# Gate and up of two SwiGLU stages as seven block products in place of eight, with feed-forward groups of six tiles

## The chip, the core and the metric

The kernel runs on one core of a Trainium2 chip. The metric is the device time of one execution in microseconds (us). The core has five engines that run side by side: TensorE (PE, matrix products; its weight loads are listed apart as PEld), VectorE (DVE, elementwise), ScalarE (ACT, activation functions and copies), GpSimd (POOL) and SyncE (SP, which here issues the loads from HBM). SBUF is the working memory, PSUM (eight banks of 128 x 512 f32) takes the matrix products.

## What is computed

A decoder trunk of two layers on 512 tokens with 1024 channels: a convolution module, attention into 256 memory tokens and a SwiGLU stage in layer 0; differential attention, memory attention and a SwiGLU stage in layer 1; a final RMSNorm. The part that the change is about is the SwiGLU stage, which both layers have:

```python
def swiglu(h, w_gate, w_up, w_down):
    return (jax.nn.silu(h @ w_gate) * (h @ w_up)) @ w_down

# in each layer i, with norm_ffn a gain per channel:
x = x + swiglu(rms_norm(x, norm_ffn[i]), ffn_w_gate[i], ffn_w_up[i], ffn_w_down[i])
```

Here h is 512 x 1024, w_gate and w_up are 1024 x 2816 and w_down is 2816 x 1024. The hidden width 2816 makes 22 tiles of 128. RMS normalisation multiplies each token by a factor r that depends on the token alone, and each channel by its gain.

## The kernel before

The residual stream lies transposed in SBUF as eight tiles `xT[t]`, 128 channels x 512 tokens. A matrix product of f32 values is made from three products of rounded values: `split` (lines 219 to 223) and `weights` (lines 208 to 217) divide a tile into a high part, cast by ACT, and a low part, the difference, made by DVE or (with `lo=G`) by POOL. `mm3` (lines 231 to 234) then multiplies high by high, high by low and low by high into the same PSUM bank. So a product of a 128 x 128 weight tile with a 128 x 512 activation tile is three matmuls, each with a weight load of its own.

The stages follow each other as `conformer` (phases c, c2), `memory_attention(0)` (m0), `ffn0` (f0), `diff_attention` (d), `memory_attention(1)` (m1) and `ffn1` (f1), lines 1041 to 1052. Each phase has its own plan of SBUF slots and PSUM banks (lines 69 to 96): a name in `SLOTS` or `BIG` owns a ring of buffers, and a buffer is used again when its last reader is done. The order of the instructions on each engine is made when the program is built, by a planner that simulates the program's time line (line 1092); `tc.issue_after` and `tc.keep_in_program_order` bind it. Each engine then works through its own list in order: an instruction that waits holds up all that stand behind it on that engine.

A SwiGLU stage before the change: `residual_out` (lines 340 to 347) ends the memory attention. For each of its eight output tiles it adds to `xT[m]`, squares for the norm and splits gain times `xT[m]` into `xg`; `norm.finish()` sums the squares over channels on PE, takes the root (small DVE operations, `rsqrt_sums`), and spreads the factor over the partitions on PE (`R`). `gate_up` (lines 622 to 634) takes `xg` without the token factor and multiplies by `R` afterwards: for each hidden tile t, 24 matmuls of 512 columns for gate and 24 for up, with a load of 512 KB each, then on DVE gate times R, up times R, their product with Silu, and a split into `a`. The 22 tiles go in groups of 8, 8 and 6 (`FFN_GROUPS`, line 37). After each group `ffn0` multiplies its part of w_down and adds to `xT`; `ffn1` does the same with tokens on the partitions (`xo`, transposed once after the first group), and ends with the final norm and the stores. In f0 the first group is followed in program order by `rotary_tables`, `minus_lambda` and `half_masks` (lines 639 to 642), which `diff_attention` needs later.

Of the kernel before, what the change touches and what calls it, by code (L numbers as in the profile page):

```python
# [17 lines left out]
AF = mybir.ActivationFunctionType  # L18
# [4 lines left out]
P = 128  # L23
# [13 lines left out]
FFN_GROUPS = [list(range(0, 8)), list(range(8, 16)), list(range(16, 22))]  # L37
# [10 lines left out]
def _pieces(value, bits, count):  # L48
# [23 lines left out]
MEMB = {"e": 4, "sq": 1, "mo": 16}  # L72
FFN0B = {"tg": 3, "sg": 3, "tu": 4, "ta": 4, "sq": 2, "ctab": 2, "stab": "ctab", "lq": 2, "lpr": "lq", **TABLES}
FFNB = {"tg": 3, "sg": 3, "tu": 4, "ta": 4, "sq": 2, "gf": 2, "xo": 8}
# [3 lines left out]
    "c": CONV, "c2": CONV, "m0": {"mkf": 8, **MEMB}, "m1": {"fetch": 4, **MEMB}, "f0": FFN0B, "f1": FFNB,  # L78
# [3 lines left out]
FFNG = {"st": 4, "wh": 3, "wl": 3, "a": 11}  # L82
# [7 lines left out]
FFNP = {"": "01234567"}  # L90
# [9 lines left out]
def trunk(ctx, tc, xt, memt, rows, taps, pos, norm_final, conv_w_pw1, conv_w_pw2, w_k_shared, w_v_shared,  # L100
# [99 lines left out]
    def pc(name, i=0):  # L200
        c = COL[name] + i
        return prm[:, c:c + 1]
# [16 lines left out]
    def split(src, name, shape=(P, 512), lo=None):  # L219
        h, l = pair(name, shape)  # L220
        A.copy(h, src)  # L221
        (lo or V).tensor_tensor(l, src, f(h), op=ALU.subtract)  # L222
        return h, l
# [17 lines left out]
    def at(pair, *idx):  # L241
        return pair[0][idx], pair[1][idx]
# [51 lines left out]
    def broadcast_rows(r, ps):  # L294

        for i in range(NB):
            ins = T.transpose(ps[:, i * P:(i + 1) * P], r[:, i:i + 1].to_broadcast([P, P]), ident)
        return ins.ins
# [41 lines left out]
    def residual_out(W, ins, norm, bias=None, cols=1, lo=None):  # L340
# [6 lines left out]
        norm.finish()  # L347
# [218 lines left out]
    def memory_attention(L, n, nxt):  # L566
        sc = small("sc", [P, NB])
        V.tensor_scalar(sc, n.r, 1.0 / 16.0, None, op0=ALU.mult)
        o, mv = [], []

# [48 lines left out]
        residual_out(mem_w_o[L], o, nxt)  # L619


    def gate_up(L, n, fts):
        a = []
        for t in fts:
            pg, pu = bank("gu"), bank("gu")
            linear(ffn_w_gate[L], t, n.xs, pg, lo=G)
            linear(ffn_w_up[L], t, n.xs, pu)
            tg, sg, tu, ta = tl("tg"), tl("sg"), tl("tu"), tl("ta")
            V.tensor_tensor(tg, pg, n.R, op=ALU.mult)  # L629
            A.activation(sg, tg, AF.Silu)  # L630
            V.tensor_tensor(tu, pu, n.R, op=ALU.mult)  # L631
            V.tensor_tensor(ta, tu, sg, op=ALU.mult)
            a.append(split(ta, "a"))
        return a

    def ffn0(n, nxt):
        for fts in FFN_GROUPS:
            a = gate_up(0, n, fts)
            if fts is FFN_GROUPS[0]:
                cur["tables"] = rotary_tables()  # L640
                cur["nlam"] = minus_lambda()
                cur["halves"] = half_masks()
            for m in range(KT):
                ps = bank("down")
                linear(ffn_w_down[0][fts[0] * P:(fts[-1] + 1) * P, :], m, a, ps)
                V.tensor_tensor(xT[m], ps, xT[m], op=ALU.add)
                if fts is FFN_GROUPS[-1]:
                    nxt.add(m, xT[m])
        nxt.finish()

    def ffn1(n):
# [4 lines left out]
        xo = [[tl("xo") for _ in range(2)] for _ in range(NB)]  # L656
# [4 lines left out]
        for fts in FFN_GROUPS:  # L661
            a = gate_up(1, n, fts)
            if fts is FFN_GROUPS[0]:
                for c in range(2):
                    for i in range(NB):
                        ps = bank("tr")
                        for t in range(4):
                            T.transpose(ps[:, t * P:(t + 1) * P], xT[4 * c + t][:, i * P:(i + 1) * P], ident)
                        A.copy(xo[i][c], ps)
            last, nk = fts is FFN_GROUPS[-1], len(fts)  # L670
            for c in range(2):
                pss = [bank("fin") for _ in range(NB)]
                w = []
                for k in range(0, nk, 2):
                    r0 = (fts[0] + k) * P
                    w.append(weights(ffn_w_down[1][r0:r0 + 2 * P, c * 512:(c + 1) * 512]))

                def product(i, k, z=ALLP, ps=None):
                    mm3t(ps or pss[i][:, z], at(a[k], ALLP, slice(i * P, (i + 1) * P)),
                         at(w[k // 2], ALLP, k % 2, z), k == 0, k == nk - 1)  # L680
# [16 lines left out]
                xg.append([tl("tu" if c else "ta") for _ in range(NB)])  # L697
# [406 lines left out]
```

## Time and profile before

| | us |
|---|---|
| median of 3 runs (lowest to highest) | 1497.13 (1496.84 to 1500.41) |
| the profiled execution's own time | 1498.82 |
| its span in the profile | 1497.0 |
| granted TensorE clock, mean | 0.995 of full speed |
| busy: PE, PEld, DVE, ACT, POOL | 1477.6, 1215.0, 887.6, 604.7, 344.5 |

The profile follows one execution. A busy time is the union of an engine's instructions. Matmuls overlap in the profile: a matmul of 512 columns is listed with 390 ns, yet the next one starts about 230 ns after it. So the rate of PE is read from the chain of waits (the work that ended last, followed back from the end), where a run of n matmuls is given with the time that it took, or from starts in the timeline. Durations on DVE and ACT overlap a little too: three DVE operations of 0.69 us each stand in the timeline as one piece of 1.88 us.

### The profile page before, as it was taken

Reading aid. Unit: us, or ns where it says so; the run is one execution under the profiler, and the core shown is the slowest. Engines: PE = TensorE matmul, PEld = TensorE weight load, DVE = VectorE, ACT = ScalarE, POOL = GpSimd, SP = SyncE. Lnnn points to the kernel's source line nnn. Section 1 sums busy time; section 2 is a strip of 40 time slices with the busy share of each in tenths; the row PEclk is TensorE's granted clock in tenths of the full one; section 3 lists DMA queues with packets and bytes.
Section 4 is the critical chain, followed back from the end, with each engine's and each line's share of the span. In section 5 each row is a group of like instructions: output and inputs, shape, how many; then the busy total and the mean of one; then the engine's idle time right before and its main releaser. Section 6 shows DMA issues by size and latency. Waiting matters only on the chain.

```text
span 1497.0 us, 18610 instructions
## 1 busy us (share of the span) xinstructions
PE 1477.6 (99%) x7258; PEld 1215.0 (81%) x7258; DVE 887.6 (59%) x1437; ACT 604.7 (40%) x980; POOL 344.5 (23%) x201
## 2 busy tenths in 40 slices
PE   8999999999999999999999999999999999999998
PEld 7888877887888888888887878788878888888886
DVE  6999966555744245334678878775465433442454
ACT  6656765444422222222425545544353232321232
POOL 2998875100220122021000000110012202210212
PEclk8999999999999999999999999999999999999999
DMA  8444272212433333332322211322143322333321
GB/s 244 119 143 134 83 210 74 71 57 70 117 99 92 92 99 99 96 88 81 100 87 70 62 53 57 113 85 71 43 125 93 105 86 85 99 99 90 101 91 57
DMA packets 231832, 143.60 MB, mean 96 GB/s; under 512 B 5568, under 2 KB 217664, under 8 KB 231744
## 3 DMA queue, kind: packets, MB, share of 16 engines
q1 hardware_dynamic: 230448, 141.58, 31.8%
q8 instruction: 57, 0.93, 0.3%
q10 hardware_dynamic: 1296, 0.84, 0.2%
q14 instruction: 31, 0.25, 0.0%
HBM read 138.20 MB, written 4.19 MB: 95 GB/s over the span
## 4 chain that ended last, share of the span: by engine, by line
PE 95%; DVE 2%; ACT 1%; issue 1%; DMA 0%; POOL 0%; SPq 0%; POOLq 0%; DVEq 0%; ACTq 0%
PE ps_gu L118 32%; PE ps_out L118 10%; PE ps_down L118 8%; PE ps_fin L118 8%; PE ps_lin L118 6%; PE ps_pw L118 6%; PE ps_mk L118 3%; PE ps_mv L118 3%; PE ps_q L118 3%; PE ps_v L118 3%; PE ps_k L118 2%; PE ps_s L118 2%; PE ps_part L118 2%; PE ps_mo L118 2%; PE ps_ms L118 1%; PE ps_st L118 1%
## 5 line engine op out<-in xcount | busy, mean ns | idle before, releaser
L214 ACT CAST wh<-st 128x1024 fp32r<-128x1024 f32 (+2 forms) x255 | 263.9, 1038 | 600.2 <-issue 171.0
L118 PE MATMUL ps_gu<-xg,wh 128*128 128x512 f32 x1408 | 436.3, 390 | 0.0
L216 POOL TENSOR_TENSOR wl<-st,wh 128x1024 fp32r<-128x1024 f32 x94 | 239.8, 2556 | 668.9 <-ACT wh L214 637.4
L118 PEld LDWEIGHTS ps_gu<-xg,wh 128*128 128x128 f32 x1408 | 264.3, 188 | 60.2
L118 PE MATMUL ps_gu<-xg,wl 128*128 128x512 f32 x704 | 278.0, 395 | 0.0
L216 DVE TENSOR_TENSOR wl<-st,wh 128x1024 fp32r<-128x1024 f32 (+2 forms) x161 | 193.7, 1206 | 90.6 <-ACT wh L214 89.1
L118 PEld LDWEIGHTS ps_gu<-xg,wl 128*128 128x128 f32 x704 | 132.2, 188 | 28.2
L449 DVE SCALAR_TENSOR_TENSOR ps_conv<-u,wcol,ps_conv 128x493 f32<-128x493 f32 (+20 forms) x176 | 120.7, 730 | 6.1 <-ACT ps_conv L446 3.7
L631 DVE TENSOR_TENSOR tu<-ps_gu,R 128x512 f32<-128x512 f32 x44 | 30.4, 691 | 137.0 <-PE ps_gu L118 137.0
L118 PE MATMUL ps_fin<-wh,a 128*128 128x512 f32 (+1 forms) x364 | 111.1, 387 | 0.0
L118 PE MATMUL ps_down<-a,wh 128*128 128x512 f32 x352 | 109.6, 394 | 0.0
L222 DVE TENSOR_TENSOR a<-ta,a 128x512 fp32r<-128x512 f32 x44 | 72.1, 1639 | 23.6 <-ACT a L221 23.6
L118 PE MATMUL ps_pw<-xg,wh 128*128 128x512 f32 x256 | 82.9, 404 | 1.5 <-ACT xg L227 0.8
L118 PE MATMUL ps_out<-mo,wh 128*128 128x512 f32 x256 | 80.9, 397 | 0.9 <-ACT wh L214 0.9
L118 PE MATMUL ps_lin<-xg,wh 128*128 128x512 f32 x256 | 81.7, 395 | 0.0
L118 PEld LDWEIGHTS ps_fin<-wh,a 128*128 128x128 f32 x364 | 67.7, 188 | 15.2
L118 PEld LDWEIGHTS ps_down<-a,wh 128*128 128x128 f32 x352 | 66.1, 188 | 15.2
L629 DVE TENSOR_TENSOR tg<-ps_gu,R 128x512 f32<-128x512 f32 x44 | 30.4, 691 | 73.8 <-PE ps_gu L118 67.9
L118 PE MATMUL ps_fin<-wl,a 128*128 128x512 f32 (+1 forms) x182 | 70.3, 387 | 0.0
L118 PE MATMUL ps_down<-a,wl 128*128 128x512 f32 x176 | 68.9, 394 | 0.0
L268 POOL TENSOR_TENSOR ry<-ov,mhalf 128x4 f32<-128x4 f32 x8 | 9.5, 1184 | 247.3 <-DVE ov L990 247.3
L118 PEld LDWEIGHTS ps_pw<-xg,wh 128*128 128x128 f32 x256 | 48.3, 191 | 14.6 <-DVE xg L228 1.8
(260 smaller groups left out, 2505.8 us busy)
## 6 DMA issues: line engine op xcount, KB each, us to landing
st<-in_ffn_w_up_dram SPq DMA_DIRECT2D x44, 512.0 KB, 3.8
st<-in_ffn_w_gate_dram SPq DMA_DIRECT2D x44, 512.0 KB, 3.8
st<-in_ffn_w_down_dram SPq DMA_DIRECT2D x38, 512.0 KB, 3.8
st<-in_conv_w_pw_dram SPq DMA_DIRECT2D x23, 512.0 KB, 4.6
st<-in_mem_w_k_dram SPq DMA_DIRECT2D x16, 512.0 KB, 4.3
st<-in_mem_w_v_dram SPq DMA_DIRECT2D x16, 512.0 KB, 3.7
st<-in_mem_w_q_dram SPq DMA_DIRECT2D x16, 512.0 KB, 4.2
st<-in_mem_w_o_dram SPq DMA_DIRECT2D x16, 512.0 KB, 4.1
```

What stands on the lines that cost most here:

```text
L118: ins = nc.tensor.matmul(*args, **kw)
L214: A.copy(wh, st)
L216: (lo or V).tensor_tensor(wl, st, f(wh), op=ALU.subtract)
L222: (lo or V).tensor_tensor(l, src, f(h), op=ALU.subtract)
L268: G.tensor_tensor(y, v, mhalf[:, :n], op=ALU.pow)
L449: V.scalar_tensor_tensor(acc[:, s:], u[j][:, :S - s], wt(s), acc[:, s:], op0=ALU.mult, op1=ALU.add)
L629: V.tensor_tensor(tg, pg, n.R, op=ALU.mult)
L631: V.tensor_tensor(tu, pu, n.R, op=ALU.mult)
```

## The change

Gate and up are made for two hidden tiles at a time. The weights of the two tiles, 1024 x 256, are cut into 2 x 2 blocks (hidden tile, half of the channels) and the activations, 1024 x 512, into 2 x 2 blocks (half of the channels, half of the tokens). Strassen's scheme (in Winograd's form) makes the four output blocks from seven block products in place of eight; each block product is four k-tiles x three matmuls of 256 columns for gate and as many for up. The operands of the products are sums and differences of blocks. The seven activation operands are made once in each stage (`block_operands`), now with the token factor in them, since the scheme mixes the two halves of the tokens. The seven weight operands are made for each pair of tiles and each of gate and up (`block_weights`): four loads of 256 KB, four additions or subtractions and seven splits. The output blocks are built up in PSUM: ACT copies a bank into the next one, and later products are added to the copy (`gate_up_pair`).

The first pair of tiles in each stage is made as before with 512 columns (`gate_up_plain`), from `xg` without the token factor; the sums and the spread of the norm are put between its matmuls, in a fixed order (`finish=False`, `hooks`). The groups are 6, 6, 6 and 4 tiles. All low parts of the stage are made on DVE. Weights have a ring of 15 buffers, each holding both parts of a 128 x 512 tile; loads have a ring of 13. The weights of w_down come in loads of 256 KB. The rotary tables, minus lambda and the half masks move from f0 to the head of m0. `ffn1` keeps the transposed residual in the tiles of `xT`. `broadcast_rows` and the transposes of `ffn1` become one accumulation group per bank.

```diff
-FFN_GROUPS = [list(range(0, 8)), list(range(8, 16)), list(range(16, 22))]
+FFN_GROUPS = [list(range(0, 6)), list(range(6, 12)), list(range(12, 18)), list(range(18, 22))]
-FFNG = {"st": 4, "wh": 3, "wl": 3, "a": 11}
+FFNG = {"w": [*range(9, 21), 0, 1, 2], "a": [21, 22, *range(3, 9)], "xh": "a"}
+FFNB = {"raw": [*range(12), 29], "xop": list(range(13, 29)), "sg": [30, 31], "p5": [12], "sq": "xop"}
...
+        if L == 0:
+            cur["tables"] = rotary_tables()
+            cur["nlam"] = minus_lambda()
+            cur["halves"] = half_masks()
...
-        residual_out(mem_w_o[L], o, nxt)
+        residual_out(mem_w_o[L], o, nxt, finish=False)
...
+    def block_operands(n):
+        shape, kept = (P, 2, HS), tc.keep_in_program_order
+        def blocks(half):
+            xb = [tl("xh", (P, 2, 2, HS)) for _ in range(2)]
+            for i in range(4):
+                t = 4 * half + i
+                kept(V.scalar_tensor_tensor(xb[i // 2][:, :, i % 2, :], xT[t].rearrange("p (l c) -> p l c", l=2),
+                                            pc(*n.gain(t)), n.R.rearrange("p (l c) -> p l c", l=2),
+                                            op0=ALU.mult, op1=ALU.mult))
+            return [[xb[i][:, l] for i in range(2)] for l in range(2)]
...
+        b11, b12 = blocks(0)
+        yield operand("xop", b11)
+        both = tl("xh", (P, 2, 2, HS))
+        t = [both[:, i] for i in range(2)]
+        minus(t, b12, b11)
+        yield operand("xop", t)
+        b21, b22 = blocks(1)
+        minus(t, b22, t)
+        yield operand("xop", t)
+        yield operand("xop", b21)
+        minus(b12, b22, b12)
+        yield operand("xg", b12)
+        yield operand("xg", b22)
+        minus(b21, b21, t)
+        yield operand("xg", b21)
+
+    def block_weights(W, t):
...
+        a11 = raw(0, 0)
+        yield split(a11, "w", shape)
+        a21, a22, s1 = raw(1, 0), raw(1, 1), tl("raw", shape)
+        V.tensor_tensor(s1, a21, a22, op=ALU.add)
+        yield split(s1, "w", shape)
+        V.tensor_tensor(a21, a11, a21, op=ALU.subtract)
+        V.tensor_tensor(a11, s1, a11, op=ALU.subtract)
+        yield split(a11, "w", shape)
+        a12 = raw(0, 1)
+        yield split(a12, "w", shape)
+        yield split(a21, "w", shape)
+        V.tensor_tensor(a12, a12, a11, op=ALU.subtract)
+        yield split(a12, "w", shape)
+        yield split(a22, "w", shape)
+
+    def gate_up_pair(L, xo, t):
...
+        def product(ps, p, start):
+            for z in range(2):
+                w = next(ws[z])
+                for k in range(KT // 2):
+                    x = at(xo[p][k // 2], ALLP, k % 2)
+                    for i, (l, r) in enumerate(((0, 0), (0, 1), (1, 0))):
+                        T.matmul(ps[:, z, :], w[l][:, k], x[r], start=start and z == k == i == 0,
+                                 stop=z == 1 and k == KT // 2 - 1 and i == 2, skip_group_check=True)
+        def block(ps, j, l):
+            sg = tl("sg", (P, HS))
+            A.activation(sg, ps[:, 0, :], AF.Silu)
+            V.tensor_tensor(ps[:, 1, :], ps[:, 1, :], sg, op=ALU.mult)
+            h, lw = (z[:, l * HS:(l + 1) * HS] for z in a[j])
+            A.copy(h, ps[:, 1, :])
+            V.tensor_tensor(lw, ps[:, 1, :], f(h), op=ALU.subtract)
+        c11, p5, c12, c22, c21 = (bank("gu", [P, 2, HS]) for _ in range(5))
+        product(c11, 0, True)
+        A.copy(c12, c11)
+        product(p5, 1, True)
+        s5 = tl("p5", (P, 2, HS))
+        A.copy(s5, p5)
+        product(c12, 2, False)
+        A.copy(c22, c12)
+        product(c11, 3, False)
+        block(c11, 0, 0)
+        product(c22, 4, False)
+        A.copy(c21, c22)
+        product(c12, 5, False)
+        V.tensor_tensor(c22, c22, s5, op=ALU.add)
+        block(c22, 1, 1)
+        V.tensor_tensor(c12, c12, s5, op=ALU.add)
+        block(c12, 0, 1)
+        product(c21, 6, False)
+        block(c21, 1, 0)
         return a
...
+    def gate_up(L, n):
+        cur["pinned"] = True
+        with tc.issue_after(cur["begun"]):
+            first = [gate_up_plain(L, n, 0, {3: n.sums, 6: n.spread}), gate_up_plain(L, n, 1)]
+        cur["pinned"] = False
+        operands = block_operands(n)
+        xo = list(itertools.islice(operands, 4))
+        for fts in FFN_GROUPS:
+            a = []
+            for t in fts[::2]:
+                if t == 0:
+                    a += [finish() for finish in first]
+                    xo += operands
+                    made = cur["lo"]
+                elif t == 4:
+                    with tc.issue_after(made):
+                        a += gate_up_pair(L, xo, t)
+                else:
+                    a += gate_up_pair(L, xo, t)
+            yield fts, a
```

## Rows read from the trace of the kernel before

**Rows 1.** The page: busy us of the engines, share of the span, instructions.
```profile
PE 1477.6 (99%) x7258; PEld 1215.0 (81%) x7258; DVE 887.6 (59%) x1437; ACT 604.7 (40%) x980; POOL 344.5 (23%) x201
```

**Rows 2.** Chain of waits, stages f0 and f1: start us, us, what.
```profile
380.47 6.93 PE ps_gu L118 x30
...
388.19 9.27 PE ps_gu L118 x40
...
397.89 72.17 PE ps_gu L118 x314
470.94 44.42 PE ps_down L118 x192
515.36 88.27 PE ps_gu L118 x384
...
648.06 66.16 PE ps_gu L118 x288
...
1119.67 6.93 PE ps_gu L118 x30
...
1390.01 66.16 PE ps_gu L118 x288
```

**Rows 3.** Chain of waits, conformer: matmuls of 256 columns (ps_mk).
```profile
100.70 5.66 PE ps_mk L118 x48
```

**Rows 4.** Timeline of PE in the conformer: start us, us, what.
```profile
52.17 0.28 PE L118 MATMUL ps_mk<-memx,wl 128*128 128x256 f32 x1
52.53 0.28 PE L118 MATMUL ps_mk<-memx,wl 128*128 128x256 f32 x1
55.02 0.28 PE L118 MATMUL ps_mk<-memx,wl 128*128 128x256 f32 x1
55.36 0.28 PE L118 MATMUL ps_mk<-memx,wl 128*128 128x256 f32 x1
```

**Rows 5.** Tile ps_mk: weight loads, with ns min/median/max.
```profile
L118 PEld LDWEIGHTS ps_mk<-memx,wh x256: 187/188/192, 51.4 to 155.5; 128*128 128x128 f32 x128
```

**Rows 6.** Second group of f0: stretch, its us, busy us of PE, PEld, DVE, ACT, POOL, clock, DMA.
```profile
515.40:603.60 88.20, 88.20 (x385) 72.05 (x384) 40.25 (x39) 25.30 (x32) 19.36 (x7) 1.00 0.33 96
```

**Rows 7.** DVE groups by form: line, operation, count, busy us, mean ns, idle before.
```profile
L222 DVE TENSOR_TENSOR a<-ta,a 128x512 fp32r<-128x512 f32 x44 | 72.1, 1639 | 23.6 <-ACT a L221 23.6
L222 DVE TENSOR_TENSOR ks<-kr,ks 128x512 fp32r<-128x512 f32 x8 | 5.5, 683 | 1.0 <-ACT ks L221 1.0
L228 DVE SCALAR_TENSOR_TENSOR xg<-xT,prm,xg 128x512 fp32r<-128x512 f32 x56 | 42.4, 775 | 0.9 <-ACT xg L227 0.8
L736 DVE SCALAR_TENSOR_TENSOR red<-kper,red 128x32 f32<-128x32 f32 x12 | 4.4, 367 | 0.4
```

**Rows 8.** Timeline of DVE: operations back to back, and one of 256 columns.
```profile
350.60 1.88 DVE L343 TENSOR_TENSOR xT<-ps_out,xT 128x512 f32<-128x512 f32 x3 [2.46 <-PE ps_out L118]
1487.78 0.42 DVE L684 TENSOR_TENSOR xo<-ps_fin,xo 128x256 f32<-128x256 f32 x1 [0.24 <-PE ps_fin L118]
```

**Rows 9.** ACT groups by form, columns as in rows 7.
```profile
L221 ACT CAST a<-ta 128x512 fp32r<-128x512 f32 x44 | 27.4, 622 | 31.8 <-DVE ta L632 31.8
L534 ACT COPY mkf<-ps_mk 128x512 f32<-128x512 f32 x4 | 2.3, 578 | 0.0
```

**Rows 10.** Who waited for whom: us in total, times, longest us.
```profile
ACT wh L214 <- PE ps_gu L118: 145.1, 46, 6.1
```

**Rows 11.** Timeline of DVE at the head of f0.
```profile
383.11 1.11 DVE L764 TENSOR_TENSOR lpr<-lq 128x64 f32<-128x64 f32 x1 [4.83 <-DMA lq<-in_diff_lambda_k_dram]
388.23 0.17 DVE L279 TENSOR_SCALAR ps_st<-ps_st 128x4 f32<-128x4 f32 x1 [1.03 <-PE ps_st L118]
392.28 0.16 DVE L333 COPY rs<-ry 128x4 f32<-128x4 f32 x1
```

**Rows 12.** Stretch m0 without the end of its output product, columns as in rows 6.
```profile
262.00:353.00 91.00, 90.17 (x457) 74.64 (x455) 44.65 (x94) 38.09 (x75) 5.38 (x4) 1.00 0.18 53
```

**Rows 13.** Timeline of DVE near the end of f1.
```profile
1481.38 0.69 DVE L684 TENSOR_TENSOR xo<-ps_fin,xo 128x512 f32<-128x512 f32 x1 [5.78 <-PE ps_fin L118]
```

More of the change, by code (lines that the diff above doesn't have):

```diff
@@ L636, in ffn0, with wtile @@
-    def ffn0(n, nxt):
[L637 to L642, printed above, removed]
+        residual_out(mem_w_o[L], o, nxt, finish=False)
+    HS = S // 2
+    def wtile(src):
+        a, c = src.shape[0] // P, src.shape[1]
+        st = tl("raw", (P, a, c))
+        nc.sync.dma_start(st, src.rearrange("(a p) c -> p a c", p=P))
+        return split(st, "w", (P, a, c))
@@ new lines, in block_operands, with operand, minus @@
+    def block_operands(n):
[8 more added lines that the diff above has]
+            return [[xb[i][:, l] for i in range(2)] for l in range(2)]
+        def operand(name, tiles):
+            parts = []
+            for t in tiles:
+                parts.append(split(t, name, shape))
+                kept(cur["split"])
+            return parts
+        def minus(dst, a, b):
+            for d, p, q in zip(dst, a, b):
+                kept(V.tensor_tensor(d, p, q, op=ALU.subtract))
+        b11, b12 = blocks(0)
[13 more added lines that the diff above has]
+        yield operand("xg", b21)
@@ new lines, in gate_up_pair @@
+    def gate_up_pair(L, xo, t):
+        ws = [block_weights(W, t) for W in (ffn_w_gate[L], ffn_w_up[L])]
+        a = [pair("a") for _ in range(2)]
+        def product(ps, p, start):
[32 more added lines that the diff above has]
+        block(c21, 1, 0)
+        return a
@@ new lines, in gate_up_plain, with finish @@
+    def gate_up_plain(L, n, t, hooks={}):
+        ps = [bank("gu"), bank("gu")]
+        w = [[wtile(W[c * D // 2:(c + 1) * D // 2, t * P:(t + 1) * P]) for c in range(2)]
+             for W in (ffn_w_gate[L], ffn_w_up[L])]
+        for k in range(KT):
+            if k in hooks:
+                hooks[k]()
+            for p, v in zip(ps, w):
+                mm3(p, at(v[k // 4], ALLP, k % 4), n.xs[k], k == 0, k == KT - 1)
+        def finish():
+            sg = tl("sg")
+            V.tensor_tensor(ps[0], ps[0], n.R, op=ALU.mult)
+            A.activation(sg, ps[0], AF.Silu)
+            V.tensor_tensor(ps[1], ps[1], n.R, op=ALU.mult)
+            V.tensor_tensor(ps[1], ps[1], sg, op=ALU.mult)
+            return split(ps[1], "a")
+        return finish
@@ L655, in ffn1 @@
             nc.scalar.dma_start(gf[i], norm_final[i * 512:(i + 1) * 512].unsqueeze(0).to_broadcast([P, 512]))
-        xo = [[tl("xo") for _ in range(2)] for _ in range(NB)]
+        xo = [[xT[4 * c + i] for c in range(2)] for i in range(NB)]
         sums_all = const("sums", [P, NB, 3])
@@ L667, in ffn1 @@
                         for t in range(4):
-                            T.transpose(ps[:, t * P:(t + 1) * P], xT[4 * c + t][:, i * P:(i + 1) * P], ident)
-                        A.copy(xo[i][c], ps)
+                            T.matmul(ps[:, t * P:(t + 1) * P], xT[4 * c + t][:, i * P:(i + 1) * P], ident,
+                                     start=t == 0, stop=t == 3, is_transpose=True, skip_group_check=True)
+                        turned.append(ps)
+                    for i in range(NB):
+                        A.copy(xo[i][c], turned[i])
             last, nk = fts is FFN_GROUPS[-1], len(fts)
@@ L672, in ffn1 @@
                 pss = [bank("fin") for _ in range(NB)]
[L673 to L676, printed above, removed]
+                w = [wtile(ffn_w_down[1][t * P:(t + 1) * P, c * 512:(c + 1) * 512]) for t in fts]
                 def product(i, k, z=ALLP, ps=None):
                     mm3t(ps or pss[i][:, z], at(a[k], ALLP, slice(i * P, (i + 1) * P)),
[L680 removed]
+                         at(w[k], ALLP, 0, z), k == 0, k == nk - 1)
                 def residual(i, ps, z):
@@ L696, in ffn1 @@
                     continue
-                xg.append([tl("tu" if c else "ta") for _ in range(NB)])
+                xg.append([tl("fx") for _ in range(NB)])
                 for i in range(NB):
```

51 lines of the change are left out of this document (27 added, 24 removed).

## The prediction

> **What bounds the kernel now.** I read the page first: PE is busy for 1477.6 of 1497.0 us, the other engines far less [rows 1]. That busy time is modelled, so next I read the chain of waits, where the SwiGLU stages are runs of matmuls that follow each other with almost nothing between. In f0 gate and up take 6.93 + 9.27 + 72.17 + 88.27 + 66.16 = 242.8 us in five pieces; the five pieces of f1, of which the first and the last are shown, sum to 242.8 as well [rows 2]. Together that is 485.6 us, a third of the span, for 2 x 22 x 48 = 2112 matmuls of 512 columns: 230 ns each (88.27/384). Last I read the stretch of one group: in 88.2 us DVE is busy for 40.25, ACT for 25.3, POOL for 19.4 [rows 6]. So PE sets these stages at its streaming rate, and only fewer or shorter matmuls move them.
>
> **What the change takes from PE.** Each layer keeps 2 x 48 = 96 matmuls of 512 columns (the plain pair) and gets 10 pairs x 7 products x 24 = 1680 of 256 columns in place of 960 of 512. What a matmul of 256 columns costs is the first question. The nearest row is the memory keys in the conformer, the same three-matmul pattern with a weight load each: 48 in 5.66 us, 118 ns [rows 3]. The timeline there shows two rates: 0.36 us per three (120 ns) and 0.34 per three (113 ns) [rows 4]. I take 118, because DVE, which I expect to be loaded in the new stage, is loaded there too; 113 and 120 are the ends. After: 2 x 96 x 0.230 + 3360 x 0.118 = 44.2 + 396.5 = 440.7. **Gain 44.9 us.** At 120 ns it would be 38.2, at 113 ns 61.7: these are its bounds.
>
> A load is listed with 188 ns [rows 5], longer than the 118 between starts, so two loads are under way at a time; this is what lets the halved matmul cost half. The Trainium skill, page "TensorE: Matmul & The Clock Gate", section "Back-to-back issue gap", speaks against the change: it holds that in a stream of weight loads and matmuls the spacing is set by both, and gives 81 ns at 128 columns and 131 at 512, so that half the columns would cost well over half the time. Here the rows show 118 against 230, so the sum goes by them, and what the rule says is rival (d).
>
> **The block scheme in the steady pairs.** PE needs 168 x 0.118 = 19.8 us per pair. DVE must fit beside it. Its operations of 512 columns are listed with 683 ns [rows 7], but back to back three take 1.88 us, so 0.60 each; one of 256 columns is 0.42, back to back about 0.33 (estimate, the same 0.09 of overlap) [rows 8]. Per pair DVE has 2 x (7 low parts + 4 sums) = 22 operations of 512 columns, 13.2 us; eight of 256 in the four blocks, 2.7; two additions of P5, 1.2. Sum 17.1 of 19.8 us. POOL no longer works in these stages: the split of `a` that took 1639 ns against 683 for the same form elsewhere [rows 7] should fall to the latter. ACT: 14 casts at 0.62, four bank copies at 0.58 [rows 9], and eight half-width operations, some 0.4 each (estimate, from DVE's half width): 8.7 + 2.3 + 3.2 = 14.2 us. Both fit. A bank copy has one whole product, 24 x 0.118 = 2.8 us, between the product that it copies and the one that adds to the copy; its 0.58 is hidden unless ACT's list holds it up. The down product of a group of six (144 x 0.231 = 33.3 us) asks DVE for 12 splits and 8 additions only, 12 us, so there DVE fills the ring of 15 weights ahead and starts the next group with 14 tiles, a pair, in hand. Steady pairs: 0.
>
> **The entry.** Here the cover is thin. Let 0 be the start of gate and up. The plain pair takes 96 x 0.230 = 22 us. The sums come after 18 matmuls (4.1 us); from the first small operation to the end of the chain took 392.28 - 388.23 = 4.2 us [rows 11] with other work between; the spread is hooked in after 36 matmuls (8.3), so `R` is there at about 10. From then DVE owes the operands: 8 multiplications at 0.775 less overlap (5.5), 8 differences (4.8), 14 low parts (8.4), 18.7 us; the plain pair's ends, 8 x 0.6 = 4.8; the first block pair's weights, 13.2, of which I let 4 be done before 10 (half of what the seven ring buffers left beside the plain pair's eight would hold); two blocks, 1.9. Sum 34.6: DVE is ready for the seventh product at 44.6. PE would reach it at 22 + 6 x 2.8 = 38.8, call it 39. That is 5.6 us late. Then the second block pair's weights may start only behind the last operand (`issue_after(made)`): to its third product DVE owes 7.2 us of weights and 3.2 of blocks, ready at 55.0, where PE would come at 44.6 + 2.8 + 5.6 = 53.0: 2 late. **7 us per layer** rounded down, 14 in all. From below: 0 if the planner puts more of the weights ahead of `R`; from above 14 per layer, if each of the 14 low parts also waits for its cast (0.5 each).
>
> **The rest.** One more change of group per layer: between group and down the chain is closed (515.36 follows 470.94 + 44.42) [rows 2]; 0 to 1 each, I take 1 in all. Loads: twice as many, half as large; POOL's and SP's lists only lose waits that PE never saw: 0. The rotary tables and lambda move to m0: some 43 small DVE operations (the largest group 12 x 367 ns [rows 7]) and a DVE wait of 4.83 us for the load of `lq` [rows 11], which in f0 cost PE nothing. In m0 DVE is busy for 44.65 of 91 us [rows 12], so there is room, but DVE stands in the softmax chain there, and whatever is behind the `lq` wait on DVE waits too: 0 to 5, I take 1, since half of the time is free; that covers the activation and the loads which go to ACT's list with them, the two memsets on POOL's and the eight transposes on PE's, which f0 no longer has. The tail: the last group has four tiles, so a token block comes every 12 matmuls in place of 18, 1.4 us sooner; DVE was idle for 5.78 us ahead of such a block [rows 13], so it keeps up; 0 to 2, I take 1.
>
> **Sum**, against the profiled execution: 1498.8 - 44.9 + 14 + 1 + 1 + 1 = 1470.9. That execution is 1.7 us above the median of 1497.1 and inside the spread of the three, so I take a little off: **1470 us**.
>
> **Rivals.**
> (a) Full cover: the planner hides the entry, and the small terms are 0: 1498.8 - 44.9 + 1 = 1455. For it: DVE is at half load in m0 [rows 12], so weights could be made early. Against: the operands can't start before `R`, so what can be moved ahead of it is weights alone.
> (b) DVE is the bound of the block pairs: its operations don't overlap across waits on ACT, so a pair costs 22 x 0.683 + 8 x 0.42 + 2 x 0.683 = 19.8 plus some 2.7 of waits (four blocks, 0.7 for each hand-over between ACT and DVE). Later groups hide 3 x 2.7 behind the pair in hand; the first has none: 2 x 2.7 more per layer, and two us for the operands: 1470.9 + 2 x 7.4 = 1486. For it: many hand-overs. Against: DVE at half load now.
> (c) Slower than before: ACT's list holds up the bank copies. Casts that wait for a weight buffer to be freed by PE wait 145.1 us in 46 times now, 3.15 in the mean and 6.1 at most [rows 10]. A bank copy behind such a cast would be ready 3.15 + 0.58 us after its product, 0.9 later than its cover of 2.8; with three such copies in each of 20 pairs that is 54 us: 1470.9 + 54 = 1525. It makes the kernel slower from 28/60 = 0.47 us per copy on. Against: the waiting casts cost PE nothing now, and the ring grows from 3 to 15.
> (d) The weight load sets the pace: a matmul of 256 columns starts only when its load of 188 ns [rows 5] is through. 3360 x 0.188 + 44.2 - 485.6 = +190, so 1498.8 + 190 + 17 = 1706; it makes the kernel slower from 131 ns per matmul on ((485.6 - 44.2)/3360). Against it stand the 118 of rows 3. The page of the Trainium skill named above stands behind this rival; by its figures, read halfway between 128 and 512 columns, the new matmul would cost three quarters of the old one (an estimate).
> (e) The columns are saved but the time isn't: the rate is 120 (+6.7), the entry at its upper end (+14) and m0 too (+4): 1470.9 + 24.7 = 1495.6, no difference.
>
> **How the numbers follow.** Forecast 0.48 (1461 to 1480), (a) 0.20, (b) 0.19, (c) 0.09, (d) 0.01, (e) 0.03. A difference of 0.3%, 4.5 us, is about what a measurement of this kernel can tell. Faster: 0.48 + 0.20 + 0.19 = 0.87; same 0.03; slower 0.10. The range reaches over (a), with a rate of 113 to 118 partly granted, and over (b): 1451 to 1489, leaving out (c) to (e), 0.13, and the far ends of the first two.
>
> **What would show it.** Right: the new `ps_gu` matmuls of 256 columns start 117 to 119 ns apart, a steady pair takes 20 us on the chain, down keeps 231 ns, and the lost time stands between 20 and 50 us behind the start of each SwiGLU stage, released by DVE. Wrong: steady pairs well over 20 us with PE released by DVE low parts (b), or by ACT bank copies (c); 150 ns and more between starts (d); a longer m0. The prediction is wrong at its root if a matmul of 256 columns doesn't cost half of one of 512.

## The result, and the profile after

The changed kernel takes 1462.95 us (median of 4 runs, 1459.59 to 1463.23), the kernel before 1497.33 in the same runs: a ratio of 0.976, 95% interval 0.974 to 0.978, so 34.4 us less. The prediction was 1470, in a range from 1451 to 1489.

The page of the profiled execution (1462.69 us, span 1460.6) answers to [rows 1]; its columns are busy us, share of the span and instructions:

```profile
PE 1435.7 (98%) x8692; PEld 1251.1 (86%) x8692; DVE 1092.0 (75%) x2007; ACT 755.9 (52%) x1419; POOL 226.1 (15%) x157
```

DVE went from 59% to 75% busy, ACT from 40% to 52%, and PE is still the engine that the chain of waits mostly runs through. The spans of the stages, each from the first matmul of its kind to the first of the next, read from the two traces:

| from, to | before | after | difference |
|---|---|---|---|
| start to the first query product of m0 | 261.9 | 263.6 | +1.7 |
| m0, to gate and up of f0 | 118.4 | 118.6 | +0.2 |
| f0, to the query product of d | 367.1 | 345.9 | -21.2 |
| d and m1, to gate and up of f1 | 372.1 | 372.0 | -0.1 |
| f1, to the end | 377.5 | 360.5 | -17.0 |

So the gain lies in the two SwiGLU stages, and only there. The chain of waits in f0 after the change (start us, us, what), which answers to [rows 2]:

```profile
382.29 4.09 PE ps_gu L119 x18
392.28 22.71 PE ps_gu L119 x135
...
481.92 44.99 PE ps_gu L119 x384
...
542.06 31.88 PE ps_down L119 x138
573.94 45.39 PE ps_gu L119 x384
...
634.85 31.90 PE ps_down L119 x138
666.75 25.49 PE ps_gu L119 x216
```

From the second group on, nothing but PE stands there. 384 matmuls of 256 columns in 45.39 us are 118 ns each, and a full group (481.92 to 573.94) takes 92.0 us, where 504 x 0.118 + 144 x 0.231 (504 matmuls of the three block pairs, 144 of the down product) gives 92.7. The piece 415 to 446 of the first group is another matter. It is made of DVE, ACT and a load of w_down; some of its rows, and what follows it:

```profile
418.79 1.19 DVE xg L223 x2
...
424.59 1.20 DVE raw L702 x2
...
438.98 5.79 DMA raw<-in_ffn_w_down_dram
...
445.46 5.32 PE ps_down L119 x22
450.78 5.72 PE ps_gu L119 x48
```

That the chain runs through DVE doesn't mean that PE stood still: matmuls of the down product are placed between the products of the second block pair, as the timeline of PE up to 447 us shows (start us, us, what, idle before and its releaser):

```profile
435.36 1.80 PE L119 MATMUL ps_down<-a,w 128*128 128x512 f32 x7
436.99 0.40 PE L119 MATMUL ps_gu<-xop,w 128*128 128x256 f32 x2
437.47 4.18 PE L119 MATMUL ps_down<-a,w 128*128 128x512 f32 x17
441.49 2.75 PE L119 MATMUL ps_gu<-xop,w 128*128 128x256 f32 x22
445.46 1.89 PE L119 MATMUL ps_down<-a,w 128*128 128x512 f32 x7 [1.22 <-ACT w L222]
```

The gain in columns alone is 22.5 us per layer by the prediction's count (half of 44.9). f0 gave 21.2, of which 0.9 are the eight table transposes and the gap around them that moved to m0; so 2.2 us were lost. f1 gave 17.0, so 5.5 were lost. These two are remainders and hold all that happened in a stage. Read directly, the first groups lost more: from the first product of gate and up to the first of the second group f0 took 99.6 us (382.13 to 481.75) and f1 106.8 (1100.07 to 1206.86). By the prices 0.230, 0.118 and 0.231 a first group is 95.0; f1 has 3.4 of transposes in it, as before, and the kernel before lost 1.2 us (f0, the tables apart) and 1.3 (f1) at the same place. That leaves 3.4 in f0 and 7.1 in f1. Most of the difference from 2.2 and 5.5 came back in later groups: the matmuls of 256 columns started 116.5 ns apart in the second group of both stages, 118.1 in the third and 117.5 in the fourth.

In the first groups PE waited for this (who, for whom: us in total, times, longest), first f0, then f1; waits under 0.3 us are left out:

```profile
PE ps_down L119 <- ACT w L222: 1.2, 1, 1.2
PE ps_gu L119 <- ACT ps_gu L741: 0.4, 1, 0.4
```

```profile
PE ps_gu L119 <- ACT ps_gu L746: 1.9, 1, 1.9
PE ps_gu L119 <- DVE w L223: 0.8, 1, 0.8
PE ps_gu L119 <- ACT ps_gu L741: 0.4, 1, 0.4
```

Most of what PE stood still for is put down to ACT, and the longest waits end 63 us (f0) and 62 us (f1) behind the start of the stage. Where f1 lost more, the timeline of ACT and PE up to 1163 us shows (same columns):

```profile
1155.98 1.14 ACT L222 CAST w<-raw 128x512 fp32r<-128x512 f32 x2 [0.88 <-DMA raw<-in_ffn_w_down_dram]
...
1159.51 2.18 ACT L222 CAST w<-raw 128x512 fp32r<-128x512 f32 x4 [2.12 <-DMA raw<-in_ffn_w_down_dram]
...
1161.60 0.57 ACT L746 COPY ps_gu<-ps_gu 128x512 f32<-128x512 f32 x1
...
1162.22 0.98 PE L119 MATMUL ps_gu<-xg,w 128*128 128x256 f32 x6 [1.90 <-ACT ps_gu L746]
```

ACT waits for loads of w_down, the bank copy c12 to c22 (line 746) stands behind those casts in its list, and PE waits for the copy. Then the clock falls: stretch, us, busy us of PE, PEld, DVE, ACT, POOL, granted clock, DMA share, GB/s:

```profile
1157.00:1162.20 5.20, 3.32 (x26) 2.99 (x26) 4.65 (x9) 3.08 (x8) 0.00 (x0) 1.00 0.87 283
1162.90:1166.30 3.40, 3.40 (x21) 3.40 (x20) 2.27 (x4) 2.85 (x6) 0.00 (x0) 0.63 0.90 264
1167.20:1180.00 12.80, 12.80 (x78) 11.42 (x78) 10.46 (x19) 5.99 (x13) 0.00 (x0) 1.00 0.22 63
```

PE was busy for 3.32 of the 5.2 us before, and the clock is at the lower of its two levels (1.2 GHz) for most of the middle stretch. The 48 matmuls from 1162.22 on take 7.48 us, against 48 x 0.118 = 5.7: 1.8 us more.

### The profile page after: what moved, and what is told of

The parts are those of the page before. It is cut to its first block, busy times and chain, and to the rows that moved or that the text cites. A ratio compares the mean times of both kernels' runs of the same rounds, so it can differ in the third digit from the quotient of the medians.

```text
span 1460.6 us, 22798 instructions
## 1 busy us (share of the span) xinstructions
PE 1435.7 (98%) x8692; PEld 1251.1 (86%) x8692; DVE 1092.0 (75%) x2007; ACT 755.9 (52%) x1419; POOL 226.1 (15%) x157
## 4 chain that ended last, share of the span: by engine, by line
PE 89%; DVE 6%; DMA 2%; issue 1%; ACT 1%; POOL 0%; SPq 0%; POOLq 0%; DVEq 0%; ACTq 0%
PE ps_gu L119 27%; PE ps_out L119 9%; PE ps_fin L119 8%; PE ps_down L119 8%; PE ps_lin L119 6%; PE ps_pw L119 6%; PE ps_mk L119 3%; PE ps_v L119 3%; PE ps_mv L119 3%; PE ps_q L119 3%; PE ps_k L119 2%; PE ps_s L119 2%; PE ps_part L119 2%; PE ps_st L119 2%; PE ps_ms L119 2%
## 5 line engine op out<-in xcount | busy, mean ns | idle before, releaser
L222 ACT CAST w<-raw 128x512 fp32r<-128x512 f32 x384 | 234.1, 621 | 222.2 <-PE ps_fin L119 65.6
L223 DVE TENSOR_TENSOR w<-raw,w 128x512 fp32r<-128x512 f32 x384 | 258.8, 687 | 98.4 <-ACT w L222 94.3
L119 PE MATMUL ps_gu<-xop,w 128*128 128x256 f32 x1920 | 232.9, 280 | 1.6 <-ACT ps_gu L741 0.8
L119 PEld LDWEIGHTS ps_gu<-xop,w 128*128 128x128 f32 x1920 | 229.8, 189 | 3.8 <-ACT ps_gu L741 1.3
L119 PE MATMUL ps_gu<-xg,w 128*128 128x256 f32 (+1 forms) x1632 | 223.2, 295 | 1.9 <-ACT ps_gu L746 1.9
L119 PEld LDWEIGHTS ps_gu<-xg,w 128*128 128x128 f32 x1632 | 210.7, 191 | 11.6 <-ACT ps_gu L746 2.1
L215 ACT CAST wh<-st 128x1024 fp32r<-128x1024 f32 (+1 forms) x121 | 125.2, 1040 | 153.8 <-PE ps_lin L119 27.4
L119 PE MATMUL ps_down<-a,w 128*128 128x512 f32 x528 | 124.7, 393 | 1.3 <-ACT w L222 1.2
L119 PE MATMUL ps_fin<-w,a 128*128 128x512 f32 (+1 forms) x540 | 124.5, 388 | 0.0
L455 DVE SCALAR_TENSOR_TENSOR ps_conv<-u,wcol,ps_conv 128x499 f32<-128x499 f32 (+20 forms) x176 | 119.9, 731 | 3.6 <-ACT ps_conv L452 1.1
L119 PE MATMUL ps_lin<-xg,wh 128*128 128x512 f32 x256 | 81.1, 394 | 0.0
```

What stands on the lines that cost most here:

```text
L119: ins = nc.tensor.matmul(*args, **kw)
L215: A.copy(wh, st)
L223: cur["split"] = (lo or V).tensor_tensor(l, src, f(h), op=ALU.subtract)
L455: V.scalar_tensor_tensor(acc[:, s:], u[j][:, :S - s], wt(s), acc[:, s:], op0=ALU.mult, op1=ALU.add)
```

## The experiments

All ran against the kernel before, three rounds each. The theory: the gain is the halved matmul times the saved eighth of the products, and what it doesn't reach is DVE's work at the entry. Line numbers in the text are those of the changed kernel; lines that an edit adds move the numbers in that run's own trace. The two SwiGLU stages together, f0 + f1 of the profiled execution, took 706.4 us in the changed kernel; this sum is the measure where a few us matter, since other stages move a little from kernel to kernel. The sums are of the rounded columns and good to 0.2 us. Each is of one execution, and how far it moves between two executions of one kernel was not measured.

| kernel | median us | f0 | f1 | f0 + f1 |
|---|---|---|---|---|
| changed kernel | 1462.95 | 345.9 | 360.5 | 706.4 |
| half the dose on DVE | 1465.94 | 346.6 | 363.6 | 710.2 |
| full dose on DVE | 1503.42 | 366.8 | 370.6 | 737.4 |
| dose in the first block pair | 1463.34 | 345.0 | 358.8 | 703.8 |
| first pair's low parts on POOL | 1462.38 | 344.2 | 358.9 | 703.1 |
| copy of line 750 on DVE | 1460.97 | 345.1 | 358.6 | 703.7 |
| copy of line 746 on DVE | 1464.53 | 344.5 | 362.3 | 706.8 |
| first pair's weights held back | 1475.98 | 353.3 | 366.5 | 719.8 |
| down product held back | 1471.46 | 352.7 | 362.8 | 715.5 |
| both reliefs | 1460.37 | 344.3 | 358.9 | 703.2 |

**All tiles plain.**

```diff
...
-                elif t == 4:
-                    with tc.issue_after(made):
-                        a += gate_up_pair(L, xo, t)
-                else:
-                    a += gate_up_pair(L, xo, t)
+                pair_ = first if t == 0 else [gate_up_plain(L, n, t), gate_up_plain(L, n, t + 1)]
+                a += [finish() for finish in pair_]
```

> All 22 hidden tiles of both stages are made in the plain way with 512 columns; the rest of the change stays (groups of six, all low parts on DVE, small loads, norm between the matmuls). Theory (the gain is the saved columns): the 45.0 us of columns come back and the 8 us lost at the two entries go, so 1463 + 45 - 8 = 1500, within 1494 to 1503, no difference from before. Rival (the rest of the change gives the gain: POOL no longer slows DVE, the norm costs less, the groups are better): 1480 or less.

Measured: 1504.5 us, ratio to before 1.0047 (1.0032 to 1.0063). All of the rest of the change together brings nothing, and this kernel is 7.4 us slower than the one before. The block products alone are worth 41.5 us (1504.5 - 1463.0) if these 7.4 belong to the rest of the change, and 34 if they don't. The rival falls. The result is 1.5 us above the theory's bound. In the profiled run 4.1 of the excess stand ahead of m0, in a part of the kernel that only the edit of `broadcast_rows` reaches, and 3.9 from d on (753.5 against 749.6 for d, m1 and f1); m0 and f0 together are as before, 485.8 against 485.5 (the planner starts some products of f0 within m0, so the two are taken as one). What makes the first two was not settled.

**The same, with each matmul from the third hidden tile on in two halves.**

```diff
...
-                mm3(p, at(v[k // 4], ALLP, k % 4), n.xs[k], k == 0, k == KT - 1)
...
+                for z in range(2):
+                    for i, (l, r) in enumerate(((0, 0), (0, 1), (1, 0))):
+                        T.matmul(p[:, z * HS:(z + 1) * HS], v[k // 4][l][:, k % 4], n.xs[k][r][:, z * HS:(z + 1) * HS], ...)
```

> As the run with all tiles plain, but each matmul of the tiles from the third on is cut into two of 256 columns, with a weight load each; the same products are computed. Theory (a matmul of 256 columns costs half of one of 512, 118 against 230 ns): 1920 matmuls become 3840, 453 us in place of 442, so 0 to 20 us above the plain run, some 1508. Rival (a fixed part or the weight load sets the pace, 150 ns or more): 3840 x 0.150 = 576, 134 us or more above the plain run.

Measured: 1515.06, which is 10.6 us above the plain run; 11.5 were worked out. The chain of waits in the second group of f0, first of the plain run, then of this one:

```profile
485.66 66.80 PE ps_gu L119 x288
```

```profile
483.82 68.21 PE ps_gu L119 x576
```

Twice the matmuls, twice the weight loads, 1.4 us more: 232 ns a matmul of 512 columns (66.80/288) against 118 for one of 256 (68.21/576). This settles the price on which the whole change rests, with the same operands on both sides. The rule of the Trainium skill ("TensorE: Matmul & The Clock Gate", "Back-to-back issue gap"), that the weight load shares in setting the spacing, does not show at 256 columns.

**The groups alone, in the kernel before.**

```diff
-FFN_GROUPS = [list(range(0, 8)), list(range(8, 16)), list(range(16, 22))]
+FFN_GROUPS = [list(range(0, 6)), list(range(6, 12)), list(range(12, 18)), list(range(18, 22))]
```

> The kernel before with groups of 6, 6, 6 and 4 hidden tiles alone. Theory (a change of group costs nothing and the tail is bound by the end of the norm, not by the number of tiles in the last group): 1497, within 2 us. The prediction on record had 2 us more for both. Rival (smaller groups give part of the gain): 1490 or less.

Measured: 1502.76, ratio 1.0036 (1.0023 to 1.0049): 5.6 us slower, which neither side had expected. f0 is as before (366.8 against 367.1), so a change of group costs PE nothing. f1 is 2.8 longer, of which 2.7 lie behind the last matmul (10.0 against 7.3 us to the end), and d with m1 is 3.1 longer, though the edit doesn't touch them. The planner orders everything anew; that this makes the difference was not shown. In the changed kernel neither shows (7.3 us of tail, 372.0 for d and m1).

**More work for DVE in the steady pairs.** The half dose has 5 in place of 9.

```diff
-        V.tensor_tensor(s1, a21, a22, op=ALU.add)
+        for _ in range(9 if t >= 6 else 1):
+            V.tensor_tensor(s1, a21, a22, op=ALU.add)
```

> The changed kernel with the first of the four sums of the weights written eight more times for each block pair from the third hidden pair on in each layer (16 more DVE operations of 0.6 us a pair, 9.6 us; the result is the same). DVE was busy for 50.2 of 60.2 us in the three pairs of the second group and for 17.2 of 31.8 in its down product. Theory (the down product is DVE's reserve, the ring lets it run a pair ahead): a full group asks DVE for 67.4 + 28.8 = 96 us of 92, so 4 us more per full group and some 5 in the last, 13 per layer: 1463 + 26 = 1489, within 1475 to 1505. Rival (no reserve, each pair waits for its own weights): 16.7 + 9.6 = 26.3 against 20.0 us a pair, 6.3 more for 16 pairs, 1463 + 101 = 1564.

> Half of the dose before: the sum written four more times, 8 more DVE operations (4.8 us) for each block pair from the third hidden pair on. With it a full group asks DVE for 67.4 + 14.4 = 82 us of 92, but a single pair for 21.5 against PE's 20.0. Theory (the down product is DVE's reserve): the two SwiGLU stages together within 5 us of the changed kernel's 345.9 + 360.5. Rival (each pair waits for its own weights): 1.5 us for each of 16 pairs, 24 us longer. The full dose made the two stages 31 us longer; in proportion, without a threshold, half of it would be 15.

Measured: with the half dose f0 + f1 is 3.8 us longer, with the full dose 31.0; the theory had at most 5 and some 26, the rival 24 and 101. A loss in proportion would have been 15 at half the dose, so there is a threshold. It lies between a group's sum of 81 us of DVE (measured, below) and 96 (worked out for the full dose) and so fits PE's 92; where in between was not tried. The second group of f0 in the changed kernel and then with the half dose (stretch, us, busy us of PE, PEld, DVE, ACT, POOL, clock, DMA):

```profile
481.90:542.10 60.20, 60.20 (x512) 59.91 (x511) 50.18 (x90) 38.30 (x76) 0.00 (x0) 1.00 0.45 132
542.10:573.90 31.80, 31.80 (x140) 25.82 (x139) 17.17 (x28) 8.09 (x14) 0.00 (x0) 1.00 0.18 51
```

```profile
481.90:542.10 60.20, 60.20 (x505) 59.66 (x504) 56.70 (x103) 35.77 (x72) 0.00 (x0) 1.00 0.42 124
542.10:573.90 31.80, 31.80 (x147) 26.14 (x147) 24.38 (x43) 9.66 (x18) 0.00 (x0) 1.00 0.23 66
```

DVE goes from 67.4 to 81.1 of 92.0 us, part of the added work moves into the down product, and the group ends at the same time. With the full dose the whole kernel is 40.5 us longer, of which 10.5 stand in d and m1, again without an edit there.

**More work for DVE in the first block pair alone.**

```diff
-        V.tensor_tensor(s1, a21, a22, op=ALU.add)
+        for _ in range(5 if t == 2 else 1):
+            V.tensor_tensor(s1, a21, a22, op=ALU.add)
```

> The changed kernel with the sum of the weights written four more times in the first block pair alone: 8 more DVE operations, 4.8 us, at the entry of each layer. Theory (at the entry PE waits for DVE, and some of the down product fills in): f0 and f1 together 5 to 10 us longer than 706.4. Rival (the entry is set by ACT's list or the loads, DVE has room): 0 to 2 us longer.

Measured: 1463.34, f0 + f1 2.6 us shorter, m0 3.1 longer. The experiment did not reach the stretch that it was meant for. The sums ran before the stage began, at the end of m0 (chain of waits, part):

```profile
339.45 2.95 DMA raw<-in_ffn_w_gate_dram
...
342.49 0.70 DVE raw L703
...
343.22 0.70 DVE raw L703
...
346.61 0.69 DVE mo L223
...
347.35 37.55 PE ps_out L119 x154
```

DVE waits there for the load of the gate weights, and the split of `mo`, which the output product of m0 needs, stands behind the sums in its list. All eight added sums run before the first product of f0. That the two stages are 2.6 us shorter is no gain from the edit: most of it (1.7 us) is in f1, where PE waited 1.6 us for the copy of line 746 and the clock stayed at 1.00 behind it. It taught where the first block pair's weights are made, and led to the next.

**The first block pair's weights held back.** `n.rooted` is the root of the norm, which stands just ahead of the spread `R`.

```diff
+                elif t == 2:
+                    with tc.issue_after(n.rooted):
+                        a += gate_up_pair(L, xo, t)
```

> The changed kernel with the first block pair's loads, weights and products held behind the root of the norm. In the changed kernel seven of its fourteen weight splits and five of its eight sums, 7.2 us of DVE, are made before it, where the sum on record had let 4 us be. Theory (what is made ahead is what keeps the entry cheap): these 7.2 us come into the stretch in which DVE is late, so f0 and f1 together are 6 to 14 us longer than 706.4. Rival (the entry isn't set by DVE's work): within 2 us.

Measured: 1475.98, f0 + f1 13.4 us longer, inside the theory's 6 to 14. PE now waits for the operands in f0 (columns as above), 27 to 38 us behind the start of the stage:

```profile
PE ps_gu L119 <- DVE xop L223: 3.3, 3, 1.8
PE ps_gu L119 <- ACT xop L222: 2.5, 1, 2.5
```

A part is the clock: in f1, where PE was busy for 11.38 of the 17 us from 1133 to 1150, it was 0.70 in the mean.

What DVE makes ahead of `R` in the changed kernel stands in its groups between 346 and 391 us (count, busy us, mean ns, idle before), of 15 weight splits eight the plain pair's, and, for f0, in the timeline just before:

```profile
L223 DVE TENSOR_TENSOR w<-raw,w 128x512 fp32r<-128x512 f32 x15 | 9.6, 683 | 0.1
...
L710 DVE TENSOR_TENSOR raw<-raw,raw 128x512 f32<-128x512 f32 x2 | 1.4, 683 | 0.0
...
L702 DVE TENSOR_TENSOR raw<-raw,raw 128x512 f32<-128x512 f32 x1 | 0.7, 682 | 0.0
L704 DVE TENSOR_TENSOR raw<-raw,raw 128x512 f32<-128x512 f32 x1 | 0.7, 682 | 0.0
L705 DVE TENSOR_TENSOR raw<-raw,raw 128x512 f32<-128x512 f32 x1 | 0.7, 682 | 0.0
```

```profile
343.00 0.69 DVE L702 TENSOR_TENSOR raw<-raw,raw 128x512 f32<-128x512 f32 x1 [1.47 <-DMA raw<-in_ffn_w_gate_dram]
343.73 0.69 DVE L704 TENSOR_TENSOR raw<-raw,raw 128x512 f32<-128x512 f32 x1
344.46 0.69 DVE L705 TENSOR_TENSOR raw<-raw,raw 128x512 f32<-128x512 f32 x1
345.07 0.68 DVE L223 TENSOR_TENSOR w<-raw,w 128x512 fp32r<-128x512 f32 x1
```

Together these are eight splits of the block pair and all of its eight sums, 16 x 0.60 = 9.6 us, more than the seven splits and five sums, 7.2 us, that the expectation had.

**The down product of the first group held back.**

```diff
...
-                    mm3(ps, at(w[k // 2], ALLP, k % 2, slice(m % 2 * P, (m % 2 + 1) * P)), a[k], ...)
+                    with tc.issue_after(cur["last"]) if fts is FFN_GROUPS[0] else ExitStack():
+                        mm3(ps, at(w[k // 2], ALLP, k % 2, slice(m % 2 * P, (m % 2 + 1) * P)), a[k], ...)
```

`cur["last"]` is the last matmul of a block product; the product of `ffn1` is held in the same way.

> The changed kernel with the down product of the first group in each layer held behind the last block product of that group, so that none of its matmuls stands between the products of the second block pair (46 of them, 10.6 us, do so in f0 now, and 6 with 20 transposes in f1). Theory (those matmuls fill PE while DVE is late, and are why the entry lost 2 to 6 us and not 7 a layer): f0 and f1 together 4 to 10 us longer than 706.4. Rival (DVE is on time by then, nothing was filled): within 2 us.

Measured: 1471.46, f0 + f1 9.1 us longer, 6.8 of it in f0, where 46 matmuls had stood in between, and 2.3 in f1, where six had. The stretch in f0 that was covered before:

```profile
441.00:451.00 10.00, 8.06 (x43) 7.86 (x43) 7.74 (x14) 4.36 (x8) 0.00 (x0) 0.68 0.86 254
```

PE stands still for 2 of 10 us, against 1.2 in the changed kernel (PE 8.78 busy, clock 1.00), and the clock was at its lower level (1.2 GHz) for much of the rest. Over the first group of f0 PE waited 1.9 us for DVE's weight splits, for which it had not waited before, and 1.9 for the copy of line 746. So the number isn't DVE's lateness alone; ACT's list and the clock are part of it.

**Relief at the entry.** Two edits, and both together; a third moved another copy.

The first, with `lo` in all seven splits:

```diff
-        shape = (P, KT // 2, P)
+        shape, lo = (P, KT // 2, P), G if t == 2 else None
...
-            yield split(a11, "w", shape)
+            yield split(a11, "w", shape, lo)
```

> The changed kernel with the 14 low parts of the first block pair's weights in each layer on POOL in place of DVE (8.4 us of DVE less at the entry). Theory (the entry is late for DVE's work): the two stages lose less than their 8 us now, 345.9 + 360.5 becomes 402 or so, 1459 in all. Rival (POOL slows DVE when both work, as 1639 ns against 683 for one form in the kernel before, and its operations are four times as long): no gain, 1463 to 1470.

```diff
-        A.copy(c21, c22)
+        (V.tensor_copy if t == 4 else A.copy)(c21, c22)
```

> The changed kernel with one bank copy (the last, c22 to c21, of the second block pair in each layer) on DVE in place of ACT. In f1 this copy came 1.57 us late behind casts that waited for a load of w_down, and PE then ran for 3.4 us at half clock, 2 us more. Theory (head of line on ACT): f1 becomes 3 us shorter, 357.5. Rival (DVE is itself the late one there, and the copy waits in its list): f1 unchanged within 1 us, or longer.

```diff
-        A.copy(c22, c12)
+        (V.tensor_copy if t == 4 else A.copy)(c22, c12)
```

> The changed kernel with the bank copy c12 to c22 (line 746) of the second block pair in each layer on DVE in place of ACT. The trace of the changed kernel names this copy for the wait of 1.57 us in f1, behind which PE ran at half clock; the run that moved the copy of line 750 had moved the wrong one. Theory (ACT's list held it, behind casts that waited for a load of w_down): f1 3 us shorter than 360.5, some 357.5. Rival (DVE's list is no earlier there): f1 within 1 us of the 358.6 that the run with the other copy had, or longer.

> Both reliefs together: the low parts of the first block pair's weights on POOL, and the copy c12 to c22 of the second block pair on DVE. Theory: f0 344 as with POOL alone, f1 356, 1459 in all, 3 to 5 us below the changed kernel. Rival (each moves the lateness to the next list): 1462 to 1464.

Measured: with the low parts on POOL the two stages are 3.3 us shorter, the theory having 4.4 (its 402 stands for 702); the whole kernel is not measurably faster (1462.38 against 1462.95). A gain from this edit is not shown: the dose in the first block pair, which relieved nothing, was 2.6 shorter, and in both the clock did not fall in f1. What is left for POOL is at most some 0.8 us in f0 (344.2 against 345.0 in that run). POOL's low parts took 1774 ns each, 2.6 times the 683 of DVE and not four times, and some of DVE's own operations were slower beside them (in f0 the splits of `xop` 886 ns against 683), so the rival is there in small. The copy of line 750, named wrongly for the late one, comes with 2.7 less: PE's wait on line 746, 1.90 us in the changed kernel (not 1.57, as the expectations have it), was a little shorter and the clock did not fall in f1. The copy of line 746 itself gains nothing. The wait went to the next instruction behind the same casts, the evacuation of the transposes (line 840), in the timeline of that run:

```profile
1163.37 0.62 ACT L222 CAST w<-raw 128x512 fp32r<-128x512 f32 x1 [0.67 <-DMA raw<-in_ffn_w_down_dram]
1163.90 1.55 ACT L840 COPY xT<-ps_tr 128x512 f32<-128x512 f32 x3
...
1164.53 0.80 PE L119 MATMUL ps_fin<-w,a 128*128 128x512 f32 x1 [3.50 <-ACT xT L840]
```

So ACT's list is held up by the loads of w_down, and what stands behind them changes with each edit. No run made these loads earlier, so what they cost in all is open. Both reliefs together give 1460.37, ratio 0.9748 (0.9734 to 0.9763) against 0.9761 (0.9742 to 0.978) of the changed kernel: 2.6 us lower, but the intervals overlap, so a better version is not shown.

## Why the prediction was right

**The columns.** The step on which it rested held: 118 ns per matmul of 256 columns was taken from [rows 3], 118 was measured (384 in 45.39 us; 116.5 to 118.1 by groups). The run with halves shows the same price on the same operands, and the plain run the worth of the block products, 34 to 41.5 us with the losses at the entries in it. Rival (d) is out by 118 against 188 (in its estimate 256 columns lie a third of the way from 128 to 512, not halfway; its three quarters belong to the third); (e) is out too, since neither the rate nor the entry nor m0 came to its upper end. That two weight loads under way at a time are what lets the halved matmul cost half, as the prediction says, fits these prices, but no run tried it.

**The steady pairs** cost nothing beyond their columns, as predicted. DVE was put at 17.1 us a pair and was busy for 16.7 per pair in their stretch (50.18/3); ACT was put at 14.2, with 12.8 (38.30/3). Over a whole group, with the weights that are made ahead during the down product, DVE took 67.4 us where the prediction's terms give 63.3 (3 x 17.1 + 12); 92.0 are there. Rival (b) had the right engine, but the down product is its reserve: the half dose left the steady groups unharmed and the full dose passed the threshold. The 0.7 us for each hand-over that (b) added stands in no row. Rival (c) is in the trace in small: of 60 copies three held up PE, that of line 741 in the second block pair by 0.4 us in each layer, and that of line 746 in f1, behind casts that wait for a load and not for a weight buffer. Rival (a), 1455, in which the planner hides the entry, came half true in size: 1463 lies midway between it and the forecast.

**The entry** is the term that was mis-sized: 14 us for both layers. Measured were 7.7 as a remainder and 10.5 read directly (3.4 in f0, 7.1 in f1). Two covers were not counted in full. The prediction let 4 us of the first block pair's weights be made before `R`, half of what the ring holds; the trace shows eight splits and eight sums, 9.6 us. And it let PE wait for DVE in the second block pair, where the planner puts the down product of the tiles that are ready: 46 matmuls, 10.6 us, in f0. Without anything made ahead (the counted 4 us too) the stages are 13.4 us longer, without the second cover 9.1.

So the sign that the prediction gave for the entry, lost time between 20 and 50 us behind the start, released by DVE, did not come. DVE's work is what would hold PE there, as the run with the weights held back shows, but with the covers PE's longest waits stand at 62 and 63 us and are put down to ACT, behind loads of w_down. In f1 the loss was as forecast in size, 7.1 against 7, for other reasons, in the main: 2.5 us of waits for ACT, 0.8 for DVE, and 1.8 of lower clock. That agreement is luck, and some of the good fit of the whole number with it.

**The small terms.** One us each had been put on the changes of group, on m0 and on the tail. Measured: none on the groups (in the run with the groups alone f0 is as before), 0.2 on m0 (with 0.9 of transposes that f0 no longer has, so nothing), none on the tail (7.3 us behind the last matmul in both). The 1.7 us ahead of m0 were in no term; this part, which of all the edits only that of `broadcast_rows` reaches, took 260.2 and 261.9 us in the two kernels without the change and 263.0 to 266.0 in all others, and why is open.

**The sum.** In the profiled executions 1498.8 - 1462.7 = 36.1 us: 45.0 of columns, less 7.7 of entries and 1.7 ahead of m0, plus 0.9 for the transposes that left f0, less 0.2 and plus 0.1 for m0 and for d with m1, is 36.4, the difference of the spans. The 7.7 were worked out as a remainder, so that this sum closes is no check of it.

## What to carry to other kernels

Before a scheme that saves multiplications, read what the smaller matmul costs from rows of the same pattern, and check that the engine that makes the operands fits into the sum of a whole group, not of each product. At the entry of such a stage ask for each engine what can be made ahead and which ready product can fill in: in f0 an entry that was costed without them came out at twice its price (7 against 3.4). A load that lands late holds up more than its own work where an engine's list is in order: in f1 the copy of line 746 stood behind casts that waited for loads of w_down, and when the copy was moved, the next instruction in the list was the late one.

## What was not expected of the hardware

A stop of PE of less than 2 us can cost as much again through the clock, but need not. In f1, behind some 1.9 us in 5.2 without a matmul, the granted clock was 0.63 from 1162.9 to 1166.3, and 48 matmuls took 1.8 us longer. In the run with the down product held back it was 0.68 from 441 to 451. In f0 of the changed kernel a wait of 1.22 us, at 445.46, was followed by 22 matmuls of the down product and then 48 of gate and up in 5.72 us, the full rate. And with the low parts on POOL a longer wait than the changed kernel's, at the same place of f1, was followed by the full rate (timeline of PE, then the stretches before and behind its end, columns as above):

```profile
1160.92 5.99 PE L119 MATMUL ps_gu<-xg,w 128*128 128x256 f32 x48 [2.56 <-ACT ps_gu L746]
```

```profile
1155.70:1160.90 5.20, 2.66 (x21) 2.15 (x19) 5.19 (x11) 3.58 (x8) 0.00 (x0) 1.00 0.93 292
1160.90:1166.90 6.00, 5.97 (x51) 5.98 (x51) 4.73 (x9) 3.25 (x6) 0.00 (x0) 1.00 0.61 181
```

So the length of the stop alone doesn't settle it. Which stops lower the clock was not tried.
